# Forgetting attention: query blocks from last to first, the causal mask added by GpSimd, value products from the last keys

## The chip, the core and the metric

One Trainium2 chip, one of its cores. A core has TensorE (matrix products, into the accumulators in PSUM), VectorE, ScalarE and GpSimd for elementwise work, and SyncE, which here issues DMAs. Each runs its own instructions in the order in which they were queued; semaphores make one wait for another. The metric is device time in microseconds (us), lower is better, as the median of several runs.

## What is computed

Two layers of a hybrid decoder trunk on 528 positions: 16 learned meta tokens, then 512 real tokens; width 1024, float32. A layer norms its input, projects it once, and hands the columns to two groups of heads: 8 heads of *forgetting attention* (64 wide) and 4 heads of chunkwise retention (128 wide). Their outputs are concatenated, projected and added to the input; then comes a gated feed-forward part. The change lies in the forgetting attention:

```python
c = jnp.cumsum(logf, axis=1).transpose(0, 2, 1)      # per head, over positions
s = jnp.einsum('bhqd,bhkd->bhqk', q_blk, k_) * scale
s = s + c_q[..., :, None] - c_k[..., None, :]
s = jnp.where(k_pos[None, :] <= q_pos[:, None], s, -jnp.inf)
p = jax.nn.softmax(s, axis=-1)
out = jnp.einsum('bhqk,bhkd->bhqd', p, v_)
```

The 16 meta queries are one block, the 512 real queries four blocks of 128. In the second layer the meta queries' output is not needed, so that layer has the four real blocks alone.

## The kernel before

**Numbers in two halves.** Every float32 matrix is split into a high part (ScalarE rounds it to TensorE's fast format, line 143, or 192 for weights) and a low part (what is left, by VectorE on line 144, or by GpSimd or VectorE on line 195 for weights). A dense product is three matmuls a chunk (`dense_steps`, line 218): high times high, high times low, low times high. Weights are fetched by SyncE's queue (line 159) and converted about one job (128 output columns, eight chunks of work) before TensorE needs them.

**Order of the work.** TensorE's instructions stand in an order written out by hand: `layer` builds a plan, in which `merge` lays the steps of attention and retention between the chunks of dense products at given places, and `spread` spaces a list of steps evenly between two of them. TensorE keeps that order. For the other engines a scheduler decides the order when the program is built, by simulating it; work under `tc.high_priority()` goes first where several instructions are ready, and instructions under `pin` keep their program order. On the chip each queue is then fixed.

**Attention of a head pair `g` (two heads, `s` = 0 and 1).** There are four pairs a layer. `fox_steps` makes a list `todo` of (head, block): before the change, for each head, the meta block (-1, first layer alone), then blocks 0, 1, 2, 3. Block `b` sees 16 + 128 (b + 1) keys, so block 3 is the largest. The steps of each entry are:

- `scores(s, b)`: two matmuls a segment (line 511) put the scores into a PSUM bank from a pool of four (`psum_a`, tiles called `psa`); block 3 has two segments of 264 keys, so two banks. VectorE adds the triangular mask `msk` (0 or -1e30) onto the last 128 columns in PSUM (line 517). Then one VectorE instruction (line 518) subtracts the scores and the broadcast sums `bc` from zero, writes the result to `pr` and keeps each row's minimum; ScalarE exponentiates with that minimum and sums each row (line 531). `bc` holds a head's cumulative sums, the same row on all 128 partitions; it is fetched by a DMA (line 501) at the head's first block, into one of two buffers, from `cdr`, which the layer wrote to DRAM shortly before (line 403).
- `values()`, after the second scores: five transposes of the value tile (line 420, tile `pd`) into two banks, four in the first, and splits of them (lines 487, 488).
- `turn(s, b)`, three entries later: `b` + 1 transposes of 128 columns of the probabilities (line 420, tile `pr`) into one bank, then high and low halves into `pth` and `ptl` (lines 143, 144). The meta block turns on VectorE and ScalarE alone (lines 557 to 559). What sticks out over the 128-wide key tiles, the last 16 keys of each block, goes through a small VectorE transpose (line 535) and lines 565 to 567. `pr`, `pth` and `ptl` exist once, for both heads.
- `product(s)`: nine matmuls (line 584; one more for the meta queries, line 576) into one bank, over the key tiles j = 0 to 4, high and low halves (j = 4, the last 16 keys, is one matmul). Its result is gathered by lines 587 and 588. `product(0)` stands after all turns of head 0, just ahead of the first turn of head 1; `product(1)` ends the list.

Retention steps of one head (lines 672 to 793) run between these in three of the four pairs, and take banks from the same pool.

Of the kernel before, what the change touches and what calls it, by code (L numbers as in the profile page):

```python
# [10 lines left out]
F32 = mybir.dt.float32  # L11
# [19 lines left out]
NBLK = SEQ // 128  # L31
# [8 lines left out]
def hybrid_kernel(ctx, tc, x_t, w_in, w_fl, w_out, w_gate, w_up, w_down, vecs, b_fg, rope, decay, mask, ident, out_t):  # L40
    nc = tc.nc
# [12 lines left out]
    msk = const.tile([128, 128], F32, name="msk")  # L54
# [62 lines left out]
    def take(lst, key):  # L117
        t = lst[rot[key] % len(lst)]
        rot[key] += 1
        return t  # L120
# [150 lines left out]
    def at(tag, dt=F32R, shape=(128, T), bufs=None):  # L271
        return phase["att"].tile(list(shape), dt, name=tag, tag=tag, bufs=bufs)
# [200 lines left out]

    def fox_steps(g, st, ly, real):

        blocks = list(range(0 if real else -1, NBLK))
        todo = [(s, b) for s in range(2) for b in blocks]
        info = {}

        def values():  # L480
            st["v"] = [at(f"vv{s}", shape=(128, 5, 128)) for s in range(2)]
            for j0, n, p3 in transpose_into(st["vt"], KOFF):
                for s in range(2):
                    v = st["v"][s][:, j0:j0 + n]
                    a0, a1 = ROWS[s]
                    b0, b1 = ROWS[1 - s]
                    nc.scalar.copy(v[:, :, a0:a1], p3[:, :, a0:a1])
                    nc.vector.tensor_sub(v[:, :, b0:b1], p3[:, :, a0:a1], v[:, :, a0:a1].bitcast(F32))
            st["mt"] = at("mixt", F32)

        def span(b):
            nq = META if b < 0 else 128
            nk = META if b < 0 else META + 128 * (b + 1)
            return nq, nk, (0 if b < 0 else META + 128 * b)

        def scores(s, b):
            nq, nk, q0 = span(b)
            if b == blocks[0]:
                bc = at("bc", F32, bufs=2)
                hd = 2 * g + s  # L500
                nc.sync.dma_start(bc, ly["cdr"][hd:hd + 1, :].partition_broadcast(128))
                st["bc"] = bc
            bc = st["bc"]
            segs = FULL if nk == T else ((0, nk),)
            pt = take(pm_tiles, "pm") if b < 0 else p_tiles[0][:, PSTEP * b:PSTEP * b + nk]
            mins = []
            normalise()
            for c0, c1 in segs:
                sc = psum_a()
                for i, kk in enumerate(st["k"][s]):  # L510
                    nc.tensor.matmul(sc[0:nq, 0:c1 - c0], st["q"][s][:, q0:q0 + nq], kk[:, c0:c1],  # L511
                                     start=(i == 0), stop=(i == 1))
                nm = tmp.tile([128, 1], F32, name="nmax", tag="nmax", bufs=6)
                with tc.high_priority():
                    if c1 == nk:
                        diag = sc[0:nq, c1 - c0 - nq:c1 - c0]
                        nc.vector.tensor_add(diag, diag, msk[0:nq, 0:nq])
                    nc.vector.tensor_tensor_reduce(pt[0:nq, c0:c1], sc[0:nq, 0:c1 - c0], bc[0:nq, c0:c1],  # L518
                                                   -1.0, 3.0e38, ALU.add, ALU.min, nm[0:nq])
                mins.append(nm)  # L520
            nmax = mins[0]
            if len(mins) > 1:
                nc.vector.tensor_tensor(nmax, mins[0], mins[1], ALU.min)
            if b < 0:
                rsum = tmp.tile([META, 1], F32, name="rsum", tag="rsum", bufs=4)
            else:
                if (s, b) == (0, 0):
                    st["sums"] = tmp.tile([128, NBLK, 2], F32, name="sums", tag="sums")
                rsum = st["sums"][:, b, s:s + 1]
            pr = pt[0:nq, 0:nk]  # L530
            nc.scalar.activation(pr, pr, AF.Exp, bias=nmax[0:nq], scale=-1.0, accum_out=rsum)  # L531
            info[s, b] = pt
            if b == blocks[-1]:
                st["ends"] = at("pe", F32, (32, NBLK, 32), 2)
                nc.vector.transpose(st["ends"], ends(p_tiles[0])[96:128])
            if b < 0:
                info["open"] = (pr, rsum)
            elif (s, b) == todo[-1]:
                nc.vector.reciprocal(st["sums"], st["sums"])
                st["rows"] = tt("tq")  # L540
                nc.scalar.copy(st["rows"][:, 0:SEQ].rearrange("p (b s d) -> p b s d", b=NBLK, s=2),
                               st["sums"].unsqueeze(3).broadcast_to([128, NBLK, 2, 64]))

        def normalise():
            if "open" in info:
                pr, rs = info.pop("open")
                nc.vector.reciprocal(rs, rs)
                nc.vector.tensor_scalar_mul(pr, pr, rs)

        def turn(s, b):  # L550
            nq, nk, q0 = span(b)
            pth, ptl = t_tiles
            if (s, b) == todo[-2]:
                normalise()
            if b < 0:
                e = at("pm", F32, (128, 32))[64:96]
                nc.vector.transpose(e, info[s, b])
                nc.scalar.copy(pth[64:64 + META, 4, 0:META], e[0:META, 0:META])
                nc.vector.tensor_sub(pth[96:96 + META, 4, 0:META], e[0:META, 0:META], pth[64:64 + META, 4, 0:META].bitcast(F32))
                return  # L560
            for j0, n, p3 in transpose_into(info[s, b], [128 * j for j in range(b + 1)]):
                split(pth[:, j0:j0 + n, q0:q0 + nq], ptl[:, j0:j0 + n, q0:q0 + nq], p3[:, :, 0:nq])
            if b == blocks[-1]:
                e = st["ends"][0:META, :, 32 - META:32]
                nc.scalar.copy(corners(pth)[0:META, 1:], e)
                nc.vector.tensor_sub(corners(ptl)[0:META, 1:4], e[:, 0:3], corners(pth)[0:META, 1:4].bitcast(F32))
                nc.vector.tensor_sub(pth[32:32 + META, 4, SEQ:T], e[:, 3], pth[0:META, 4, SEQ:T].bitcast(F32))

        def product(s):
            mt, v, pt = st["mt"], st["v"][s], t_tiles  # L570
            a0, a1 = ROWS[s]
            b0, b1 = ROWS[1 - s]
            ol = tt("ol")
            if not real:
                po = psum_a()
                nc.tensor.matmul(po[:, 0:META], v[:, 4, :], pt[0][:, 4, 0:META], start=True, stop=True)
                with tc.high_priority():
                    nc.scalar.copy(ol[a0:a1, 0:META], po[b0:b1, 0:META])
                    nc.vector.tensor_add(mt[a0:a1, 0:META], po[a0:a1, 0:META], ol[a0:a1, 0:META])
            po = psum_a()  # L580
            for j in range(5):
                c0 = max(0, KOFF[j] - META)
                for i, pp in enumerate(pt if j < 4 else pt[:1]):
                    nc.tensor.matmul(po[:, c0:SEQ], v[:, j, :], pp[:, j, META + c0:T],  # L584
                                     start=(j == 0 and i == 0), stop=(j == 4))
            with tc.high_priority():
                nc.scalar.copy(ol[a0:a1, META:T], po[b0:b1, :])
                nc.vector.tensor_add(mt[a0:a1, META:T], po[a0:a1, :], ol[a0:a1, META:T])
            if s == 1:

                rb = psum_a()
                for b in range(NBLK):
                    nc.tensor.transpose(rb[:, 128 * b:128 * b + 128], st["rows"][:, 128 * b:128 * b + 128], idt)
                nc.vector.tensor_mul(mt[:, META:T], rb, mt[:, META:T])
                mh, ml = mix_tile(2 * (g % 2))
                split(sv(mh, real), sv(ml, real), sv(mt, real))
                st["mix"] = (mh, ml)

        steps = []
        n = len(todo)  # L600
        lag = 3
        for i in range(n + lag):
            if i < n:
                steps.append(lambda a=todo[i]: scores(*a))
            if i == 1:
                steps.append(values)
            if i >= lag:
                s, b = todo[i - lag]
                if s == 1 and b == blocks[0]:
                    steps.append(late(lambda: product(0)))  # L610
                steps.append(lambda a=(s, b): turn(*a))
        steps.append(lambda: product(1))
        cut = len(steps) - lag - 1
        return steps[:cut], steps[cut:]
# [810 lines left out]
```

## Time and profile before

| what | value |
|---|---|
| runs shown (median, lowest, highest) | 1272.59 us (1272.03 to 1273.82), 3 runs |
| span of the profiled execution, first to last instruction | 1270.1 us |
| median of the runs less that span | 2.5 us |
| TensorE busy | 1252.6 us (99%) |
| VectorE busy | 1003.8 us (79%) |
| ScalarE busy | 694.5 us (55%) |
| GpSimd busy | 263.3 us (21%) |
| mean granted TensorE clock | 0.996 of full speed |

The profiled execution has no time of its own beside its span; the span is compared with the median. A row of a group reads: line, engine, operation, tiles (out<-in), shape, count, busy time, mean of one in ns, idle time of the engine just ahead of it and what ended that. A row of the timeline reads: start, length, engine, line, operation, tiles, shape, count, and in brackets the idle time ahead of it. PE is TensorE's matmuls, PEld its weight loads, DVE VectorE, ACT ScalarE, POOL GpSimd, SP SyncE; SPq marks a DMA being issued. Matmuls overlap, so one may last 0.28 us while the next starts 0.12 us after it.

### The profile page before, as it was taken

What the parts mean: (1) busy time and instruction counts of PE and PEld (TensorE: products, weight loads), DVE (VectorE), ACT (ScalarE), POOL (GpSimd) and SP (SyncE); (2) the same over time, 40 slices, a digit from 0 to 9 for tenths busy, and PEclk for the clock granted to TensorE, in tenths of its full rate; (3) what the DMA queues carried; (4) which work ended last, traced back from release to release, by engine and by line L of the source; (5) the groups of instructions that cost most, each with busy time, mean ns of one, the idle gap of its engine ahead of it and who ended that gap; (6) DMA issues with size and microseconds to landing.
All of it is one profiled execution on the core that took longest, in us unless ns stands there. A gap on an engine that the chain in (4) does not pass through costs nothing.

```text
span 1270.1 us, 23589 instructions
## 1 busy us (share of the span) xinstructions
PE 1252.6 (99%) x9225; PEld 1193.1 (94%) x9225; DVE 1003.8 (79%) x1866; ACT 694.5 (55%) x1284; POOL 263.3 (21%) x524
## 2 busy tenths in 40 slices
PE   9999999999999999999999999999999999999997
PEld 8899999999999999999998989998789999999996
DVE  7877856879988888887786877568899888888867
ACT  7666556676444444444465665457764444444445
POOL 3355546420000000000025546454100000000000
PEclk9999999999999999999999999999999999999999
DMA  6322222213323232322323122221223333333321
GB/s 218 93 68 84 83 94 75 68 68 116 106 96 100 100 100 100 100 100 84 101 76 114 63 101 84 77 91 67 100 91 126 101 100 101 100 100 100 100 84 67
DMA packets 45679, 120.56 MB, mean 95 GB/s; under 512 B 5360, under 2 KB 12272, under 8 KB 45568
## 3 DMA queue, kind: packets, MB, share of 16 engines
q1 hardware_dynamic: 45136, 118.77, 28.3%
q8 instruction: 72, 1.18, 0.4%
q14 instruction: 39, 0.32, 0.1%
q10 hardware_dynamic: 432, 0.29, 0.1%
HBM read 116.91 MB, written 2.13 MB: 94 GB/s over the span
## 4 chain that ended last, share of the span: by engine, by line
PE 89%; DVE 5%; ACT 4%; DMA 1%; issue 1%; ACTq 0%; DVEq 0%; SPq 0%
PE psd L218 27%; PE psa L902 18%; PE psd L1037 14%; PE psd L902 13%; PE psa L218 5%; PE psa L1037 4%; PE psa L420 2%; PE psa L511 1%; PE psa L584 1%; PE psa L717 1%; PE psa L751 1%; DMA bc<-cdr 1%; PE psa L381 1%; ACT whi L192 1%; DVE pr L518 0%
## 5 line engine op out<-in xcount | busy, mean ns | idle before, releaser
L195 POOL TENSOR_TENSOR wlo<-raw,whi 128x128 fp32r<-128x128 f32 x504 | 259.1, 550 | 288.8 <-ACT whi L192 287.3
L218 PE MATMUL psd<-xh,whi 128*128 128x264 f32 (+1 forms) x792 | 195.6, 314 | 0.4 <-ACT whi L192 0.4
L218 PE MATMUL psd<-xl,whi 128*128 128x264 f32 (+1 forms) x792 | 186.3, 302 | 0.6 <-DVE xl L321 0.6
L218 PE MATMUL psd<-xh,wlo 128*128 128x264 f32 (+1 forms) x792 | 186.7, 303 | 0.0
L218 PEld LDWEIGHTS psd<-xh,whi 128*128 128x128 f32 x792 | 128.2, 189 | 5.2 <-ACT whi L192 0.8
L218 PEld LDWEIGHTS psd<-xh,wlo 128*128 128x128 f32 x792 | 127.0, 188 | 6.3 <-DVE wlo L195 0.6
L218 PEld LDWEIGHTS psd<-xl,whi 128*128 128x128 f32 x792 | 127.6, 189 | 5.2 <-DVE xl L321 1.2
L192 ACT CAST whi<-raw 128x512 fp32r<-128x512 f32 (+1 forms) x168 | 98.2, 613 | 45.7 <-PE psd L218 31.5
L890 ACT CAST whi<-raw 128x1024 fp32r<-128x1024 f32 (+2 forms) x62 | 54.8, 884 | 50.3 <-PE psd L902 37.0
L890 ACT CAST fwhi<-raw 128x1024 fp32r<-128x1024 f32 (+2 forms) x62 | 55.6, 897 | 47.9 <-PE psd L902 40.1
L891 DVE TENSOR_TENSOR fwlo<-raw,fwhi 128x1024 fp32r<-128x1024 f32 (+2 forms) x62 | 64.0, 1032 | 11.7 <-ACT fwhi L890 11.6
L85 POOL MEMSET kl<- 64x528 f32 x2 | 1.1, 534 | 345.5 <-PE psa L902 345.5
L891 DVE TENSOR_TENSOR wlo<-raw,whi 128x1024 fp32r<-128x1024 f32 (+2 forms) x62 | 62.9, 1014 | 12.2 <-ACT whi L890 12.1
L902 PE MATMUL psa<-th,whi 128*128 128x264 f32 (+1 forms) x232 | 65.4, 282 | 0.0
L902 PE MATMUL psa<-th,wlo 128*128 128x264 f32 (+1 forms) x232 | 65.4, 282 | 0.0
L902 PE MATMUL psa<-tl,whi 128*128 128x264 f32 (+1 forms) x232 | 65.3, 282 | 0.0
L902 PE MATMUL psa<-th,fwhi 128*128 128x264 f32 (+1 forms) x224 | 63.4, 283 | 0.0
L902 PE MATMUL psa<-tl,fwhi 128*128 128x264 f32 (+1 forms) x224 | 63.3, 283 | 0.0
L902 PE MATMUL psa<-th,fwlo 128*128 128x264 f32 (+1 forms) x224 | 63.2, 282 | 0.0
L531 ACT ACTIVATE pr<-pr,nmax 128x144 f32<-128x144 f32 (+1 forms) x64 | 36.9, 576 | 43.2 <-DVE nmax L518 31.2
L890 ACT CAST fwhi<-S 128x1024 fp32r<-128x1024 f32 x20 | 21.0, 1049 | 68.6 <-PE psa L902 66.5
L968 ACT COPY e<-psa 128x264 f32<-128x264 f32 (+1 forms) x114 | 42.9, 376 | 27.7 <-PE psa L902 23.6
(356 smaller groups left out, 4036.6 us busy)
## 6 DMA issues: line engine op xcount, KB each, us to landing
raw<-w_in SPq DMA_DIRECT2D x54, 512.0 KB, 3.5
raw<-w_gate SPq DMA_DIRECT2D x44, 512.0 KB, 4.0
fraw<-w_up SPq DMA_DIRECT2D x38, 512.0 KB, 3.4
raw<-w_down SPq DMA_DIRECT2D x64, 256.0 KB, 2.7
raw<-w_out SPq DMA_DIRECT2D x16, 512.0 KB, 3.4
raw<-w_down SPq DMA_DIRECT2D x32, 192.0 KB, 2.5
bc<-cdr SPq DMA_DIRECT2D x16, 264.0 KB, 3.4
raw<-w_up SPq DMA_DIRECT2D x6, 512.0 KB, 3.5
```

Of the source, the lines that this page charges most:

```text
L192: pin(nc.scalar.copy(hi, job["raw"][:, c0:c1]), pinned)
L195: pin(sub(lo[:, c:c + step], job["raw"][:, c0 + c:c0 + c + step], hi[:, c:c + step].bitcast(F32)), pinned)
L218: nc.tensor.matmul(ps[1][b][:, 0:c1 - c0], w[:, wk, :], x[:, c0:c1], start=(k == 0 and i == 0), stop=(k == n - 1 and i == 2))
L381: nc.tensor.matmul(ps[:, 0:c1 - c0], wf[k // HB][:, k % HB, :], st["x"][k][part][:, c0:c1], start=(i == 0), stop=(i == 2 * NK - 1))
L420: nc.tensor.transpose(ps[:, 128 * j:128 * j + 128], src[:, o:o + 128], idt)
L511: nc.tensor.matmul(sc[0:nq, 0:c1 - c0], st["q"][s][:, q0:q0 + nq], kk[:, c0:c1], start=(i == 0), stop=(i == 1))
L531: nc.scalar.activation(pr, pr, AF.Exp, bias=nmax[0:nq], scale=-1.0, accum_out=rsum)
L890: nc.scalar.copy(hi, src)
L891: nc.vector.tensor_sub(lo, src, hi.bitcast(F32))
L902: nc.tensor.matmul(bank()[:, 0:b.shape[-1]], a[:, o + k, :], b, start=(fresh and k == 0 and i == 0), stop=(k == n - 1 and i == 2), skip_gr ...
L968: nc.scalar.copy(self.t["e"][:, i], self.t["x"][:, 0:w])
L1037: nc.tensor.matmul(v[:, 0:c1 - c0], a[:, s * n + k, :], b[:, c0:c1], start=(k == 0 and i == 0), stop=(k == n - 1 and i == 2))
```

## The change

Three things. The blocks of a head go from 3 down to 0 (and to the meta block in the first layer); places that named the first, the last or a certain entry of the list are named anew. The mask is no longer added to each score tile in PSUM by VectorE: a new `mask(b)` lets GpSimd add it to the columns of `bc` that are block `b`'s own keys, at the head's start for block 3 and right after block `b`'s scores for block `b` - 1. Since later (smaller) blocks never read the columns that were masked for larger ones, one `bc` serves all blocks. And `product` runs over j = 4, 3, 2, 1, 0 where it ran 0 to 4.

```diff
-        blocks = list(range(0 if real else -1, NBLK))
+        blocks = list(range(NBLK - 1, -1 if real else -2, -1))
...
+        def mask(b):
+            nq, nk, q0 = span(b)
+            diag = st["bc"][0:nq, nk - nq:nk]
+            with tc.high_priority():
+                nc.gpsimd.tensor_add(diag, diag, msk[0:nq, 0:nq])
+
         def scores(s, b):
             nq, nk, q0 = span(b)
             if b == blocks[0]:
-                bc = at("bc", F32, bufs=2)
+                st["bc"] = at("bc", F32, bufs=2)
                 hd = 2 * g + s
-                nc.sync.dma_start(bc, ly["cdr"][hd:hd + 1, :].partition_broadcast(128))
-                st["bc"] = bc
+                nc.sync.dma_start(st["bc"], ly["cdr"][hd:hd + 1, :].partition_broadcast(128))
+                mask(b)
             bc = st["bc"]
...
                 with tc.high_priority():
-                    if c1 == nk:
-                        diag = sc[0:nq, c1 - c0 - nq:c1 - c0]
-                        nc.vector.tensor_add(diag, diag, msk[0:nq, 0:nq])
                     nc.vector.tensor_tensor_reduce(pt[0:nq, c0:c1], sc[0:nq, 0:c1 - c0], bc[0:nq, c0:c1],
                                                    -1.0, 3.0e38, ALU.add, ALU.min, nm[0:nq])
                 mins.append(nm)
+            if b > blocks[-1]:
+                mask(b - 1)
...
-                if (s, b) == (0, 0):
+                if (s, b) == todo[0]:
                     st["sums"] = tmp.tile([128, NBLK, 2], F32, name="sums", tag="sums")
...
-            if b == blocks[-1]:
+            if b == 0:
                 st["ends"] = at("pe", F32, (32, NBLK, 32), 2)
...
-            elif (s, b) == todo[-1]:
+            elif (s, b) == (1, 0):
                 nc.vector.reciprocal(st["sums"], st["sums"])
...
-            if b == blocks[-1]:
+            if b == 1:
                 e = st["ends"][0:META, :, 32 - META:32]
...
-            for j in range(5):
+            for j in range(4, -1, -1):
                 c0 = max(0, KOFF[j] - META)
                 for i, pp in enumerate(pt if j < 4 else pt[:1]):
                     nc.tensor.matmul(po[:, c0:SEQ], v[:, j, :], pp[:, j, META + c0:T],
-                                     start=(j == 0 and i == 0), stop=(j == 4))
+                                     start=(j == 4), stop=(j == 0 and i == 1), skip_group_check=True)
```

## The prediction

> **What bounds the kernel now.** I read the page's busy line, then the same shares in the stretches that hold attention (20 to 330 us in layer 0, 640 to 960 us in layer 1), then who made TensorE wait there.
>
> ```profile
> span 1270.1 us, 23589 instructions
> PE 1252.6 (99%) x9225; PEld 1193.1 (94%) x9225; DVE 1003.8 (79%) x1866; ACT 694.5 (55%) x1284; POOL 263.3 (21%) x524
> ...
> 20.00:330.00 310.00, 305.60 (x2466) 301.88 (x2465) 244.75 (x572) 196.63 (x433) 128.84 (x248) 0.99 0.26 85
> 640.00:960.00 320.00, 317.48 (x1980) 283.43 (x1979) 245.34 (x516) 197.65 (x405) 130.27 (x256) 1.00 0.26 86
> ```
> ```profile
> PE psa L584 <- DVE ptl L144: 1.7, 1, 1.7
> PE psa L511 <- DVE mixt L588: 0.7, 1, 0.7
> PE psa L511 <- DVE kl L454: 0.6, 1, 0.6
> PE psa L511 <- DVE nmax L518: 0.6, 1, 0.6
> ...
> PE psa L420 <- DVE vv L488: 1.6, 1, 1.6
> ```
>
> The columns of the two stretches are length, then busy time of PE, PEld, DVE, ACT, POOL, then granted clock. TensorE works 305.6 of 310 us and 317.5 of 320 us, and the change takes no matmul from it and adds none. So it can win only TensorE's waits, and the second fence holds nearly all of those in the attention part (the last row is layer 1, the others layer 0). VectorE has 65 and 75 us to spare in these stretches, GpSimd 181 and 190 us: work that leaves the one for the other is worth nothing by itself.
>
> The longest wait is the first product with values, 1.69 us, and TensorE's clock shows more:
>
> ```profile
> 55.50 0.59 ACT L143 CAST pth<-psa 128x512 fp32r<-128x512 f32 x1
> 56.63 0.48 PE L584 MATMUL psa<-pth,vv 128*128 128x512 f32 x1
> 58.06 0.68 DVE L144 TENSOR_TENSOR ptl<-psa,pth 128x512 fp32r<-128x512 f32 x1
> 58.79 0.51 PE L584 MATMUL psa<-ptl,vv 128*128 128x512 f32 x1 [1.69 <-DVE ptl L144]
> ...
> 75.17 0.48 PE L584 MATMUL psa<-pth,vv 128*128 128x512 f32 x1
> 75.48 0.39 PE L584 MATMUL psa<-ptl,vv 128*128 128x512 f32 x1
> ...
> 59.20:60.60 1.40, 1.40 (x8) 0.54 0.40 79
> 60.60:62.70 2.10, 2.10 (x11) 0.50 0.49 197
> ```
>
> The low half of the last block's transposed probabilities (512 columns) came at 58.74, with TensorE already there. The same pair of matmuls starts 2.16 us apart here and 0.31 us apart without a wait, so the wait is worth 1.85 us. Then the granted clock was 0.54 and 0.50 for 3.5 us: 1.40 x 0.46 + 2.10 x 0.50 = 1.69 us. Together 3.54 us, the largest thing that this change can reach.
>
> **The change, part by part.**
>
> *Order of blocks and of the product's keys.* Today the block before the product is the heaviest: four transposes (52.90 us below) and a 512-column split. Reversed, the last turned blocks are block 0 (one transpose, one 128-column split) and, in layer 0, the meta block (no TensorE work). Block 0's turn moves to where block 2's stands (50.13).
>
> ```profile
> 45.80 0.27 PE L420 MATMUL psa<-idt,pr 128*128 128x128 f32 x1
> 49.52 0.28 DVE L144 TENSOR_TENSOR ptl<-psa,pth 128x128 fp32r<-128x128 f32 x1
> 50.13 0.49 PE L420 MATMUL psa<-idt,pr 128*128 128x128 f32 x3
> 52.90 0.60 PE L420 MATMUL psa<-idt,pr 128*128 128x128 f32 x4
> ```
>
> With block 0's own lag, 45.80 to 49.80 = 4.0 us, its low half would be there at 54.1, 2.5 us before the product (56.63); the product also reads key block 0 last, some 0.8 us later still (1648 columns stand ahead of it, and layer 0's mean is 305.6 us / 2466 = 0.124 us for about 264). So this wait goes, and the half clock behind it: -3.54 us. Next in line there is the meta block's chain (normalise, transpose, split), which needs no TensorE and has about four steps, at 1.4 us each by the two turns above (50.13, 52.90: two steps); I cost it at nothing, and at 1 us if VectorE's backlog of some 4 us covers it too. The nine matmuls of a product are the same nine in another order: nothing.
>
> *Waits for a PSUM bank.*
>
> ```profile
> 240.87 0.39 PE L511 MATMUL psa<-kh,qs 128*128 128x264 f32 x1 [0.69 <-DVE mixt L588]
> ...
> 104.06 0.41 PE L218 MATMUL psd<-xh,wlo 128*128 128x264 f32 x2
> 104.62 0.41 PE L420 MATMUL psa<-idt,pr 128*128 128x128 f32 x2
> ...
> 104.39 0.16 DVE L517 TENSOR_TENSOR psa<-psa,msk 16x16 f32<-16x16 f32 x1
> ```
>
> After a product, scores waited 0.69 us for its bank. Scores of two banks follow the product today, and are replaced by a turn of one bank and a one-bank score. I take the 0.69 us as gone; bounds 0 and 0.69.
>
> *The mask leaves VectorE for GpSimd.*
>
> ```profile
> L517 DVE TENSOR_TENSOR psa<-psa,msk x72: 160/290/300, 36.7 to 863.4; 128x128 f32<-128x128 f32 x64, 16x16 f32<-16x16 f32 x8
> ...
> 20.00:330.00 310.00, 10.59 (x40) 0.99 0.26 85
> 640.00:960.00 320.00, 9.36 (x32) 1.00 0.26 86
> ...
> L195 POOL TENSOR_TENSOR wlo<-raw,whi x504: 446/463/2074, 21.6 to 897.8; 128x128 fp32r<-128x128 f32 x168
> L518 DVE CUSTOM_DVE_ANT_0 pr<-psa,bc x80: 289/432/575, 39.6 to 864.6; 128x264 f32<-128x264 f32 x32, 128x144 f32<-128x144 f32 x16, 128x272 f32<-128x272 f32 x16, 128x400 f32<-128x400 f32 x16
> ```
>
> VectorE loses 72 instructions, 10.59 + 9.36 = 19.95 us, all under TensorE's work: 0, except the start at 104.62 us above, right behind a mask's end (104.55) and 0.44 us after the matmul before it (104.18) where 0.124 is usual: -0.3. GpSimd gains 64 sums of 128x128, nearest row L195: 64 x 0.46 to 0.55 (the median and the page's mean) = 30 to 35 us, in idle time. But each sum is now a hand-over: the reduction L518 of block b must have read the columns before GpSimd masks them for b-1, and L518 of b-1 waits for that. With two hand-overs of 0.05 us (58.74 to 58.79 above) that is 0.65 us at most, and scores of one head are two steps, some 2.8 us, apart except at its start. So it hides, as long as GpSimd comes to it within about 2 us. Behind the mask on GpSimd stand the low halves of the weights (L195), converted about a job ahead, some 5 us; behind L518 on VectorE stands everything.
>
> *The start of a pair's attention.* Block 3 comes first and takes two of four banks at once, block 2 a third, the values' transposes a fourth and then a fifth. The hard places are the two layer starts, where the broadcast sums have just been fetched:
>
> ```profile
> 37.05 3.38 POOL L195 TENSOR_TENSOR wlo<-raw,whi 128x128 fp32r<-128x128 f32 x8 [5.66 <-ACT whi L192]
> 37.60 0.71 PE L420 MATMUL psa<-idt,pd 128*128 128x128 f32 x5
> 39.44 0.16 DVE L518 CUSTOM_DVE_ANT_0 pm<-psa,bc 16x16 f32<-16x16 f32 x1 [1.72 <-DMA bc<-cdr]
> 39.67 0.40 PE L511 MATMUL psa<-kh,qs 128*128 128x272 f32 x1 [0.62 <-DVE nmax L518]
> ...
> 675.95 0.31 DVE L518 CUSTOM_DVE_ANT_0 pr<-psa,bc 128x144 f32<-128x144 f32 x1 [2.95 <-DMA bc<-cdr]
> 680.09 0.30 PE L420 MATMUL psa<-idt,pd 128*128 128x128 f32 x1 [1.57 <-DVE vv L488]
> ```
>
> Layer 0: TensorE reaches the fifth transpose at 37.60 + 0.7 (1536 more columns of scores, at 0.124 us per 264) + 0.5 (four transposes of 0.12) = 38.8, and its bank is free only after block 3's first reduction, 39.44 + 0.43 + 0.1 = 40.0: a wait of 1.2 us where 0.62 stands. If the mask gets behind the eight L195 (to 40.43), the second reduction ends at 41.5 and costs 0.4 more. I take +0.8 (bounds +0.2, +2.5, the latter with a half clock again). Layer 1: by the same count the fifth transpose meets a free bank at 676.5, and the later waits for the retention's values stay; 0 (bounds -1.6, +1.5). The six other starts, where the sums are there long before: +0.8 for all, about 0.13 each (0 to 0.55, one L195, each). SyncE: the fetch of the sums still waits for a head's last reduction, now of a small block; I take 0.
>
> Sum: -3.54 - 0.69 - 0.3 + 0.8 + 0 + 0.8 = -2.9 us on the span, 1270.1 to 1267.2. The median of the runs shown, 1272.59, lies 2.5 us above the span; I carry that over: **1269.6 us**.
>
> [...]
>
> **Rivals.**
>
> *Slower: GpSimd's queue holds VectorE up.* GpSimd runs in order and waited long for ScalarE:
>
> ```profile
> POOL wlo L195 <- ACT whi L192: 287.3, 74, 32.3
> ...
> 45.81 2.07 POOL L195 TENSOR_TENSOR wlo<-raw,whi 128x128 fp32r<-128x128 f32 x4 [5.38 <-ACT whi L192]
> 47.49 0.95 DVE L627 TENSOR_TENSOR xsw<-xsw,sr 128x528 f32<-128x528 f32 x1 [0.34 <-ACT xsw L626]
> ...
> 55.51 0.71 DVE L627 TENSOR_TENSOR xsw<-xsw,sr 128x528 f32<-128x528 f32 x1 [1.29 <-ACT xsw L626]
> ```
>
> A mask placed behind a low half whose high half is late keeps L518, and VectorE behind it, waiting. If that costs TensorE one L195 (0.55 us) a head, 16 heads make 8.8 us: 1278.4. It decides from (2.9 + 2.5) / 16 = 0.34 us a head. For it: 74 waits of L195 for ScalarE. Against: VectorE's 140 us of slack, and the steps' spacing. A second brake of the same kind: L627, with two SBUF inputs, took 0.71 us alone and 0.95 beside L195, so a mask can add some 0.24 us to such an instruction; at 64 masks that is 15 us of VectorE at most, less than the 20 it loses. [...]
>
> *Same: the wait moves.* The half clock comes back at layer 0's start, where I expect 1.2 us of waiting: +1.69 us and a little more waiting give 1271.5 to 1273.5, middle 1272.6. That the reversal does nothing, since the meta block's chain is late in the old wait's place, ends there too.
>
> *Better:* all bank waits of the fence go, 1.57 and 0.62 included, and the starts cost nothing: -3.54 - 0.69 - 0.3 - 2.2 = -6.7, 1265.9.
>
> **How the numbers follow.** 0.2% is 2.5 us, about what a measurement of this kernel tells from no change: faster is under 1270.05. Likeliest case 0.42 (own range 1267.5 to 1271.5, three quarters of it faster), better 0.11, the wait moves 0.18, the clock's loss not coming back 0.03, slower 0.26. Faster 0.43, same 0.31, slower 0.26. The range 1265 to 1279 leaves out the far ends of better and of slower.
>
> **What would show it.** Right: no L584 waiting on L144 near 58 us, clock 1.00 from 55 to 66 us; no adds on VectorE at the mask's line, 72 on GpSimd near 0.46 to 0.55 us; a TensorE wait of over 1 us near 39 us. Wrong: rows of L518 waiting for GpSimd that sum to many us, TensorE waiting at scores or turns in most heads, or a slice of low clock at a layer's start.

## The result and the profile after

The changed kernel takes 1288.81 us (median, 1288.22 to 1290.69) against 1272.31 us (1271.31 to 1273.82) for the kernel before, measured beside it: a ratio of 1.0131, 95% interval 1.0117 to 1.0144. It is 16.5 us slower. Forecast was 1269.6 us, and the range ended at 1279.

The first two lines of the page after, span and busy time of each engine:

```profile
span 1288.9 us, 23656 instructions
...
PE 1259.9 (98%) x9225; PEld 1196.4 (93%) x9225; DVE 992.0 (77%) x1794; ACT 695.7 (54%) x1284; POOL 294.9 (23%) x596
```

TensorE does the same 9225 matmuls, and is busy 7.3 us longer for them (1252.6 before). Some 5 us of that are a lower clock: it is granted at 0.50 for four stretches of 3.41 us where it was one, and 3 x 3.41 x 0.5 = 5.1 us. Where the other 2 us of busy time come from isn't shown. The remaining 11.5 us of the longer span (1288.9 against 1270.1) are TensorE's waits. VectorE has 72 instructions less and GpSimd 72 more, as the diff says. The waits of VectorE and GpSimd, then those of TensorE (what waited, for what: us in total, times, longest):

```profile
POOL bc L500 <- DVE nmax L521: 25.1, 23, 4.4
...
DVE pr L521 <- POOL bc L500: 20.2, 16, 2.6
...
POOL bc L500 <- DMA bc<-cdr: 14.6, 5, 4.6
...
PE psa L420 <- DVE mixt L584: 4.1, 2, 3.0
...
PE psa L517 <- DVE ptl L144: 2.6, 3, 1.8
...
PE psa L420 <- DVE nmax L521: 2.1, 2, 1.3
...
PE psa L420 <- DVE vv L488: 1.9, 1, 1.9
...
PE psa L517 <- DVE nmax L521: 1.3, 2, 1.0
```

The 1.69 us wait of the first product is gone, as forecast. In its place stand turns that wait for a bank behind a product's meta queries (4.1 us; line 584 is the old 576's result), and scores and turns that wait for splits and reductions. Behind these stands VectorE, which waits 16 times, 20.2 us together, in the reduction (line 521, the old 518) for a mask by GpSimd (line 500). One such place, in the timeline of the changed kernel (start, length, engine, line; in brackets the idle time ahead):

```profile
746.03 2.98 POOL L195 TENSOR_TENSOR wlo<-raw,whi 128x128 fp32r<-128x128 f32 x7 [2.05 <-ACT whi L192]
...
746.44 0.43 DVE L521 CUSTOM_DVE_ANT_0 pr<-psa,bc 128x272 f32<-128x272 f32 x1
...
748.98 0.45 POOL L500 TENSOR_TENSOR bc<-bc,msk 128x128 f32<-128x128 f32 x1
...
749.46 0.31 DVE L521 CUSTOM_DVE_ANT_0 pr<-psa,bc 128x144 f32<-128x144 f32 x1 [2.58 <-POOL bc L500]
...
749.83 0.39 PE L517 MATMUL psa<-kh,qs 128*128 128x264 f32 x1 [0.96 <-DVE nmax L521]
...
752.19 0.39 PE L517 MATMUL psa<-kh,qs 128*128 128x264 f32 x1 [1.84 <-DVE ptl L144]
...
752.60:756.10 3.50, 3.50 (x13) 2.81 (x13) 2.98 (x11) 1.75 (x5) 1.80 (x4) 0.51 0.27 101
```

At 746.03 GpSimd starts seven low halves of weights (line 195), which had waited 2.05 us for ScalarE. At 746.88 VectorE has finished the larger block's reduction (746.44 and its minimum, 0.08 us, behind it), so from then on the next mask could run. It stands behind the low halves in GpSimd's queue and starts at 748.98, when the last of them is done, without a gap. VectorE stands still for 2.58 us. TensorE then waits 0.96 us at the next scores, and 1.84 us more for a split that VectorE does late. The last row is the stretch behind (length, then busy time of PE, PEld, DVE, ACT, POOL, then the granted clock): the clock is 0.51 for 3.5 us, some 1.7 us more. Twelve of the other fifteen waits of that row look the same: GpSimd comes to the mask straight from a run of low halves. The other three, 1.4 us together, are at the two layer starts, with no low half just ahead of the mask.

The second new kind of wait, from the same view:

```profile
244.63 0.16 DVE L584 TENSOR_TENSOR mixt<-psa,ol 64x16 f32<-64x16 f32 x1
...
244.94 1.08 PE L420 MATMUL psa<-idt,pr 128*128 128x128 f32 x4 [3.02 <-DVE mixt L584]
```

and two stretches behind it, in the same columns:

```profile
245.00:248.60 3.60, 3.60 (x17) 3.60 (x18) 2.90 (x6) 0.59 (x1) 0.00 (x0) 0.50 0.45 150
248.60:252.00 3.40, 3.40 (x22) 3.32 (x21) 1.15 (x4) 0.41 (x2) 0.00 (x0) 0.66 0.00 0
```

In layer 0's last pair the first head's product is followed by block 3's turn, whose four transposes need a bank. The banks are taken until VectorE has gathered the product's meta columns at 244.63, so TensorE waits 3.02 us, and its clock is 0.50 and 0.66 for 7 us: 3.6 x 0.50 + 3.4 x 0.34 = 3.0 us more. Before, this place cost 0.69 us.

The time between fixed points of TensorE's list shows where all of it went. A pair ends, in this table, with the first of the four transposes by which its row sums are turned for the scaling (tiles `psa<-idt,tq`); starts are read from each trace and subtracted. Differences to the kernel before in us, one profiled execution each (the one of the changed kernel is the slowest of its four runs, so its sum is 18.8):

| stretch | changed | mask back | order alone | meta first | first pair only |
|---|---|---|---|---|---|
| to the first scores | -0.2 | +0.1 | -0.3 | -0.1 | +0.1 |
| layer 0, pair 1 | -0.5 | -2.9 | -3.1 | -1.9 | -3.0 |
| pair 2 | +2.7 | +1.4 | +1.4 | -0.1 | -0.1 |
| pair 3 | +1.7 | -0.2 | -0.2 | +0.1 | +0.1 |
| pair 4 | +5.0 | +5.5 | +3.6 | +0.4 | 0.0 |
| to layer 1's scores | +0.5 | +0.4 | +0.6 | +1.0 | 0.0 |
| layer 1, pair 1 | +3.8 | +2.3 | +2.0 | +2.3 | 0.0 |
| pair 2 | +4.9 | 0.0 | 0.0 | 0.0 | 0.0 |
| pair 3 | +1.4 | 0.0 | 0.0 | 0.0 | 0.0 |
| pair 4 and the rest | -0.4 | +0.3 | +0.3 | +0.4 | +0.1 |

The last four columns are kernels of the experiments below.

### The profile page after: what moved, and what is told of

It reads as the page before. It is cut to its first block, busy times and chain, and to the rows that moved or that the text cites. A ratio compares the mean times of both kernels' runs of the same rounds, so it can differ in the third digit from the quotient of the medians.

```text
span 1288.9 us, 23656 instructions
## 1 busy us (share of the span) xinstructions
PE 1259.9 (98%) x9225; PEld 1196.4 (93%) x9225; DVE 992.0 (77%) x1794; ACT 695.7 (54%) x1284; POOL 294.9 (23%) x596
## 4 chain that ended last, share of the span: by engine, by line
PE 81%; DVE 7%; ACT 6%; POOL 2%; issue 2%; DMA 1%; ACTq 0%; DVEq 0%; SPq 0%; POOLq 0%
PE psd L218 23%; PE psa L907 18%; PE psd L1042 14%; PE psd L907 13%; PE psa L1042 4%; PE psa L218 4%; POOL wlo L195 2%; PE psa L420 1%; ACT whi L192 1%; PE psa L517 1%; PE psa L589 1%; PE psa L722 1%; PE psa L756 1%; PE psa L381 1%; DVE kl L454 1%
## 5 line engine op out<-in xcount | busy, mean ns | idle before, releaser
L536 ACT ACTIVATE pr<-pr,nmax 128x272 f32<-128x272 f32 (+2 forms) x64 | 36.9, 576 | 52.2 <-DVE nmax L521 34.1
L521 DVE CUSTOM_DVE_ANT_0 pr<-psa,bc 128x264 f32<-128x264 f32 (+3 forms) x80 | 33.6, 433 | 38.0 <-POOL bc L500 20.2
```

## The experiments

**Which part costs.** Three kernels undo one part each, or keep one alone; a fourth keeps the product's order alone. The masks back on VectorE:

```diff
-        def mask(b): ...                 (and its two calls)
+                    if c1 == nk:
+                        diag = sc[0:nq, c1 - c0 - nq:c1 - c0]
+                        nc.vector.tensor_add(diag, diag, msk[0:nq, 0:nq])
```

> The changed kernel with one part undone: the mask is again added to the scores in PSUM by VectorE; blocks still go from last to first, products still begin at the last keys. Theory A (the slowdown is the hand-over between VectorE and GpSimd: VectorE waited 20 us for masks): all of the 16.5 us goes, 1269 to 1274 us. Theory B (the slowdown is the order of the blocks, which asks for more PSUM banks at a pair's start and right after the product): 1283 to 1289 us. Half and half would be about 1280 us.

The product back to j = 0 to 4, masks and order as changed:

```diff
-            for j in range(4, -1, -1):
+            for j in range(5):
```

> The changed kernel with the product's key order undone (0 to 4 again); GpSimd masks and reversed blocks stay. Theories A and B: 1288 us within 2, the same nine matmuls wait for the same tiles. Theory C (the product's order costs): 1285 us or less.

The reversed blocks alone, in the kernel before:

```diff
-        blocks = list(range(0 if real else -1, NBLK))
+        blocks = list(range(NBLK - 1, -1 if real else -2, -1))
```

> The reversed order of blocks alone: VectorE masks the scores in PSUM, products go from the first keys. Theory A: 1269 to 1274 us. Theory B: 1283 to 1289 us. If the product's order matters for the reversed blocks, this differs from the kernel with both by over 1 us.

The reversed product alone, in the kernel before:

```diff
-            for j in range(5):
+            for j in range(4, -1, -1):
```

> The kernel before with the product's key order reversed alone. Theories A and B: 1272 us within 1; the long wait at the first product stays, since the first keys' low half of block 3 is late for each key tile alike. Theory C: slower than 1274 us.

Measured beside 1271.5 us of the kernel before: masks back 1276.44 us (1.0041, 1.0027 to 1.0055), product back 1288.4 us (1.0134, 1.0119 to 1.015), order alone 1276.28 us (1.0035, 1.002 to 1.0049), product alone 1271.84 us (1.0002, 0.9992 to 1.0011). "Mask back" and "order alone" fall between the ranges of theories A and B: both the masks and the order cost. The product's order does nothing, the blocks' order loses 4.8 us (1276.28 - 1271.5), and the masks the rest: "product back" differs from "order alone" by the masks only, 1288.4 - 1276.3 = 12.1 us. The table says where: the order gains 3.1 us in layer 0's first pair and loses 7 in three other places; the masks add their 12 us in six of the eight pairs.

**Is it GpSimd's work, or the wait for it?** A kernel with the masks on VectorE, as in "mask back", in which GpSimd still does the 72 additions, one a block and of the same inputs, into a tile that nobody reads:

```diff
-                nc.gpsimd.tensor_add(diag, diag, msk[0:nq, 0:nq])
+                nc.gpsimd.tensor_add(idle[0:nq, 0:nq], diag, msk[0:nq, 0:nq])
+                    (and VectorE's addition to the scores, as before)
```

> Reversed order, the mask added to the scores by VectorE, and GpSimd does the same 72 sums besides, into a tile that nobody reads. Theory A1: nobody waits for them, 1275 to 1279 us. [...]

It took 1278.12 us (1.0052, 1.0039 to 1.0066). The two pages' lines of busy time, of "mask back" and of this one:

```profile
PE 1256.3 (98%) x9225; PEld 1195.7 (94%) x9225; DVE 1004.0 (79%) x1866; ACT 695.6 (54%) x1284; POOL 262.3 (21%) x524
```
```profile
PE 1256.1 (98%) x9225; PEld 1195.4 (94%) x9225; DVE 1005.7 (79%) x1866; ACT 695.7 (54%) x1284; POOL 295.5 (23%) x596
```

GpSimd works 33.2 us more (295.5 against 262.3), VectorE 1.7 us more, and the ratios' intervals overlap. So the 72 additions on GpSimd, while nobody waits for them, do not make the 12 us: had they done so, this kernel would stand near 1288.5 us (1276.44 + 12.1). Of the up to 15 us that the prediction allowed for VectorE instructions slowed beside a mask, 1.7 us show here.

**Does it have to be GpSimd's queue?** Two kernels move the wait. In the first, VectorE itself adds the masks to the sums:

```diff
-                nc.gpsimd.tensor_add(diag, diag, msk[0:nq, 0:nq])
+                nc.vector.tensor_add(diag, diag, msk[0:nq, 0:nq])
```

> The changed kernel with one engine exchanged: the mask is added to the broadcast sums as in the change, block by block after the block before, but by VectorE. Theory A1 (the cost of the mask is that VectorE waits while GpSimd has it in its queue): near the kernel with the mask on the scores, 1275 to 1279 us. Theory A2 (the cost is the chain itself: a mask can only follow the reduction of the block before, whatever the engine): 1284 to 1289 us.

In the second, each block has its own copy of the sums, fetched and masked at the head's start, so no mask waits for a reduction:

```diff
-                st["bc"] = at("bc", F32, bufs=2)
-                nc.sync.dma_start(st["bc"], ...)
-                mask(b)
+                for a in range(NBLK - 1, -1, -1):
+                    n = span(a)[1]
+                    st["bc"][a] = at(f"bc{a}", F32, (128, n), 1)
+                    nc.sync.dma_start(st["bc"][a], ly["cdr"][hd:hd + 1, 0:n].partition_broadcast(128))
+                    mask(a)
```

> The changed kernel with the chain taken away: the sums are fetched once for each of the four blocks, and GpSimd masks each copy as soon as it has landed, a head ahead (only the meta block's mask still follows block 0). The order and the engine stay. Theory A1 and A2: VectorE's 20 us of waiting for masks fall under 6, and the time to 1274 to 1280 us. [...] If the three further fetches a head hold up SyncE's queue, VectorE waits for the fetches instead, over 1282 us.

Both stayed where the changed kernel is: 1288.2 us (1.0133, 1.0119 to 1.0147), the range of theory A2, and 1290.33 us (1.0146, 1.0128 to 1.0164), where A1 and A2 had 1274 to 1280. Their waits, first of the kernel with VectorE's masks, then of the one with a copy for each block:

```profile
DVE bc L500 <- DMA bc<-cdr: 27.4, 11, 7.9
...
PE psa L420 <- DVE nmax L521: 5.3, 3, 2.0
```
```profile
POOL bc L500 <- DMA bc<-cdr: 78.8, 31, 4.8
...
PE psd L218 <- POOL wlo L195: 4.7, 4, 2.1
...
DVE pm L524 <- POOL bc L500: 7.6, 4, 5.1
...
DVE pr L524 <- POOL bc L500: 3.0, 4, 1.2
```

In the first, GpSimd is out of it, but a head's first mask stands in VectorE's queue at the place that the scheduler gave it and waits there for the sums' fetch: 11 times, 27.4 us. In the second, VectorE's waits for masks fall only to 10.6 us, not under the 6 expected: 3.0 us at the four blocks, and 7.6 us at the meta block (tile `pm`), whose mask still follows block 0. GpSimd waits 78.8 us for the fetches (each copy's single buffer is free only after the head before); the low halves behind it come late, and TensorE waits 4.7 us for them where it waited for none. In all three forms an instruction whose input isn't there holds up what stands behind it in its queue: in the changed kernel low halves that wait for ScalarE (2.05 us at 746.03) hold up the mask, here VectorE's masks wait 27.4 us and GpSimd's 78.8 us for the fetches. But since the first landed in A2's range, these two could not tell whether the form itself (masks on the sums) is dear, so a third was made: the kernel with VectorE's masks, but a head's first block masked in the scores, so that nothing waits for the fetch ahead of its reader.

```diff
-                mask(b)                  (at a head's first block)
+                    if c1 == nk and b == blocks[0]:
+                        diag = sc[0:nq, c1 - c0 - nq:c1 - c0]
+                        nc.vector.tensor_add(diag, diag, msk[0:nq, 0:nq])
```

> The changed kernel, but VectorE itself adds the masks to the sums of every block but a head's first, and the first block's mask is added to the scores, as in the kernel before. No mask stands in GpSimd's queue and none waits for the sums' fetch. If the 12 us of the mask part belong to masks that wait in somebody's queue (for a row of low halves on GpSimd in the changed kernel, for the fetch on VectorE in the vector-masks-sums kernel), this one stands where the mask-back kernel stands: 1275 to 1279 us. If they belong to the form itself (a mask on the sums orders each head's blocks one behind the other), it stays with the changed kernel: 1284 us or more. In between: both have a share.

1278.03 us (1.0055, 1.004 to 1.007); the interval overlaps that of "mask back" (1.0041, 1.0027 to 1.0055). So A2 fails: the form costs nothing that these runs tell apart. The 10 us between 1288.2 and 1278.0 go with the first mask of each head, the one that waited for the fetch in VectorE's queue.

**The queue made short.** The low halves cut to 8 of 128 columns, in the changed kernel, in "mask back" and in the kernel before. TensorE's third product takes the high half in place of the low one, so it does as many matmuls; the output lacks the low halves' part.

```diff
-                pin(sub(lo[:, c:c + step], raw[:, ...], hi[:, c:c + step]), pinned)
+                m = 8 if job["pool"] else 128
+                pin(sub(lo[:, c:c + step, 0:m], raw[:, ..., 0:m], hi[:, c:c + step, 0:m]), pinned)
...
-                for i, (w, x) in enumerate(((hi, xh), (hi, xl), (lo, xh))):
+                for i, (w, x) in enumerate(((hi, xh), (hi, xl), (hi if pool else lo, xh))):
```

> The changed kernel, with GpSimd's row of low halves (L195) cut to 8 of 128 columns each, so that the queue ahead of its masks is nearly empty; the third product of those weights takes the high half in place of the low one, so its output lacks the low halves' part, and TensorE does as many products as before. To be read against the next kernel, which is the mask-back kernel with the same cut. If the masks' price is the wait behind the low halves, the two differ by 0 to 3 us; if it is the hand-over to GpSimd, or GpSimd's slowness as such, by about 12 us as the uncut pair does (1288.8 against 1276.4 us).

> The mask-back kernel (reversed blocks, reversed product, masks added to the scores by VectorE) with GpSimd's low halves cut to 8 of 128 columns and the high half in the third product of those weights, so its output lacks the low halves' part. Without a mask on GpSimd the low halves are early anyway, so 1274 to 1278 us is expected, by either theory; it is the base for the kernel before this one.

> The kernel before with GpSimd's low halves cut to 8 of 128 columns and the high half in the third product of those weights, so its output lacks the low halves' part. The light mask-back kernel took 1269.0 us, which was 7.4 us below the uncut one; this one tells how much of that was GpSimd's low halves for any kernel. If the cut is worth the same to the kernel before, it takes 1264 us, and the order still costs 5 us; if the order's loss itself needs the low halves, it takes 1269 to 1271 us.

Measured: changed and cut 1268.83 us (0.9981, 0.9972 to 0.9991), mask back and cut 1268.99 us (0.9984, 0.9975 to 0.9993), before and cut 1264.97 us (0.9948, 0.9931 to 0.9964). "Mask back and cut" was expected at 1274 to 1278 us, so that expectation was wrong: the cut takes some 7 us off that kernel too. Of the first, the group of low halves and the waits for masks:

```profile
L196 POOL TENSOR_TENSOR wlo<-raw,whi 128x8 fp32r<-128x8 f32 x504 | 104.2, 241 | 318.5 <-ACT whi L192 309.7 <-issue 8.7
```
```profile
POOL bc L501 <- DVE nmax L522: 53.1, 38, 4.5
...
DVE pr L522 <- POOL bc L501: 6.7, 10, 1.5
```

One low half takes 241 ns where it took 545, and a run of them is short. The masks are handed over as before, 72 times; they now wait mostly for VectorE (53.1 us), and VectorE for them 6.7 us, with no wait over 1.5. And the 12.1 us are gone: 1268.83 against 1268.99. So the hand-over as such costs nothing here; the masks' price needs the low halves around them in GpSimd's queue. The cut also shortens VectorE's own work, by 17 us (986.7 against 1004.0 us busy in the two "mask back" kernels), which eases all waits for VectorE; that the queue is how the price comes about is read from the rows of 746 to 752 us, not from the cut alone. Nor does it separate a mask that waits behind low halves from low halves that wait behind a mask; for the first speaks that TensorE's list of waits in the changed kernel has no row for GpSimd's low halves. The cut is worth 5.7 us to the kernel before as well, so the order's loss, 4.8 us uncut, is 4.0 us here (1268.99 - 1264.97): the order doesn't need the low halves for it.

**What the order loses.** The reversed blocks put block 3's turn right behind the first head's product. The kernel with the order alone has, in layer 0's last pair:

```profile
238.80 0.16 DVE L578 TENSOR_TENSOR mixt<-psa,ol 64x16 f32<-64x16 f32 x1
238.88 0.67 DVE L587 TENSOR_TENSOR mixt<-psa,ol 64x512 f32<-64x512 f32 x1
...
239.01 0.66 PE L420 MATMUL psa<-idt,pr 128*128 128x128 f32 x4 [2.41 <-DVE mixt L578]
```

a wait of 2.41 us. If that is the loss, leaving the meta rows first (meta, 3, 2, 1, 0) takes it away, since the turn behind the product is then the meta block's, without a bank:

```diff
-        blocks = list(range(NBLK - 1, -1 if real else -2, -1))
+        blocks = ([] if real else [-1]) + list(range(NBLK - 1, -1, -1))
```

> The kernel before with the blocks of a head reversed, as in the order-alone kernel (1276.3 us), except that the 16 meta rows of layer 0 stay first: meta, 3, 2, 1, 0. The first turn behind the first head's product is then the meta block's, which takes no PSUM bank. If the loss of 3.6 us in layer 0's last pair is the turn of block 3 that waits for the bank of the meta product, it goes: 1272 to 1274 us, with about +2 us left at the start of layer 1, which is not touched. If the loss comes from the reversed blocks elsewhere, it stays at 1276. If the gain of 3 us in the first pair came from the meta rows' new place, that goes too and the time is 1275 to 1279.

1273.75 us (1.0017, 1.0008 to 1.0027), within the first theory's 1272 to 1274. The same place, in this kernel's timeline:

```profile
236.22 0.16 DVE L578 TENSOR_TENSOR mixt<-psa,ol 64x16 f32<-64x16 f32 x1
...
241.46 0.60 PE L420 MATMUL psa<-idt,pr 128*128 128x128 f32 x4
```

The transposes wait for nothing, and the stretch costs 0.4 us where it cost 3.6; pair 2 has lost its 1.4 us too. What stays is the start of layer 1, +2.3 us. There the fifth transpose of the retention's values waits for a bank that still holds the attention's transposed values, until ScalarE and VectorE have split those (lines 487 and 488). First rows of this kernel, then its clock in the stretch behind, then that of the kernel before:

```profile
678.17 0.63 ACT L530 ACTIVATE pr<-pr,nmax 128x400 f32<-128x400 f32 x1
...
678.91 0.49 ACT L487 CAST vv<-psa 128x256 fp32r<-128x256 f32 x2
...
679.32 0.56 DVE L488 TENSOR_TENSOR vv<-psa,vv 128x256 fp32r<-128x256 f32 x2 [1.19 <-ACT vv L487]
...
680.75 0.30 PE L420 MATMUL psa<-idt,pd 128*128 128x128 f32 x1 [1.90 <-DVE vv L488]
```
```profile
681.70:685.10 3.40, 3.40 (x13) 2.71 (x12) 3.02 (x10) 2.33 (x8) 0.00 (x0) 0.50 0.13 41
```
```profile
681.70:685.10 3.40, 3.40 (x26) 3.14 (x25) 2.87 (x10) 2.18 (x5) 1.52 (x3) 1.00 0.22 59
```

Before, that wait was 1.57 us and no clock was lost. VectorE isn't what is late: it stands still for 1.19 us until ScalarE starts the split at 678.91. ScalarE does the exponentials of blocks 3 and 2 just ahead of it (0.73 and 0.63 us), where before it was block 1's alone (0.52 us). The wait is 1.90 us, and the clock falls to 0.50 for 3.4 us: 1.7 us, most of the 2.3.

**The gain alone.** The order gains in one pair and loses in others, so a last kernel reverses the blocks in layer 0's first pair and leaves all else as before:

```diff
+        if g == 0 and not real:
+            blocks.reverse()
```

> The kernel before with the blocks reversed in one pair alone, the first of layer 0, masks and product as before. In the run with the order alone that pair was 3.05 us shorter and the others longer or alike. If pairs are independent: 3 us off the span, 1268 to 1269.5 us against 1271.5 us. Rival: what the order saves there comes back in the pairs behind it, 1271 us or more.

1268.96 us beside 1270.51 us of the kernel before, ratio 0.998, interval 0.9971 to 0.9988: 0.2% faster, and within the expected 1268 to 1269.5. Its first product, and its clock behind it:

```profile
57.51 0.48 PE L586 MATMUL psa<-pth,vv 128*128 128x512 f32 x1
...
57.83 0.39 PE L586 MATMUL psa<-ptl,vv 128*128 128x512 f32 x1
```
```profile
59.00:66.00 7.00, 7.00 (x61) 6.86 (x60) 6.16 (x19) 5.65 (x14) 4.95 (x10) 1.00 0.35 113
```

The high and the low half's matmuls start 0.32 us apart, the clock stays 1.00, and the pair is 3.0 us shorter.

## Why the prediction was wrong, step by step

- *Order, first product, -3.54 us:* right in mechanism and nearly in size. The wait and the half clock go, and the first pair alone gains 3.0 us of its table row. In the changed kernel the masks take 2.4 us of it back in the same pair (-0.5, against -2.9 in "mask back"); a turn there waits 1.04 us for the meta product's bank.
- *Bank behind a product, -0.69 us:* this step failed. "Scores of two banks follow the product today, and are replaced by a turn of one bank and a one-bank score" overlooked that the turn which stood there, the meta block's, takes no bank at all. In its place came waits of 4.1 us, the longest (3.02) with 3.0 us of clock behind it. With the order alone it is one wait of 2.41 us, and "meta first" takes it away.
- *The mask, -0.3 us, and its hand-over hidden:* the step that failed most. "So it hides, as long as GpSimd comes to it within about 2 us" was a condition, and the sum went on as if it held. It counted the low halves that stand behind a mask in GpSimd's queue, not those ahead of it. GpSimd came up to 2.6 us late, TensorE ran out of work meanwhile (0.96 and 1.84 us at the place shown), and the masks cost 12.1 us where the sum had -0.3. The slack of VectorE, 140 us in sum, was no argument, since the wait falls where TensorE's next step hangs on VectorE.
- *Layer 0's start, +0.8 us (wait of 1.2 us where 0.62 stood):* right within 0.2 us. The changed kernel waits 1.29 and 0.35 us there, 1.0 us more than before.
- *Layer 1's start, 0 (-1.6 to +1.5):* too low. The order alone costs 2.0 us, the changed kernel 3.8. The prediction had the retention's values wait as before; they wait 0.33 us longer in "meta first" (1.90 against 1.57), behind ScalarE's larger exponentials, and behind that the clock was 0.50 for 3.4 us; the bound had no half clock in it, though the argument for layer 0 did.
- *The six other starts, +0.8 us for all:* not told apart from the bank waits by any run; with the order alone four of the six show nothing, and with "meta first" none loses over 0.4 us.
- *The product's order, 0:* right (1.0002).
- *The rival "GpSimd's queue holds VectorE up":* this is what happened, at a chance of 0.26. It put one low half, 0.55 us, on a head; VectorE's waits were 20.2 / 16 = 1.3 us a head, since a mask stands behind a run of low halves (seven at 746.03) rather than one, and TensorE lost 12.1 / 16 = 0.76. The masks alone leave the range (1269.6 + 12.1 = 1281.7); the order's 4.8 us, which no rival had, come on top.
- *The clock:* the prediction counted 1.69 us of half clock behind a wait of 1.69 us, and gave 0.03 to "the clock's loss not coming back", a loss that stays when the wait goes. It went with the wait: in "first pair only" the clock is 1.00 from 59 to 66 us, where the kernel before has a mean of 0.76, and the pair is 3.0 us shorter, more than the 1.85 us that the wait alone was worth. At layer 1's start in "meta first" a wait of 1.90 us had 0.50 for 3.4 us behind it.

## What to carry to other kernels

An instruction given to an idle engine is not free when another engine's next instruction waits for it (12.1 us here, for 72 additions of 0.46 us in the median): count what can stand ahead of it in that engine's queue (here a run of four to eight low halves, about 2 to 4 us), not the engine's busy share, and ask what the waiting engine holds up in turn. When steps are reordered, write down for each what it takes from a shared pool at its new place; a step that took nothing and made room for a late one is easily lost. And where a reordering gains in one known place, change that place alone.

## What was not expected of the hardware

Two waits at one place differ little, and the clock behind them much: behind 1.57 us of waiting (the kernel before, layer 1) it stayed 1.00, and behind 1.90 us at the same place ("meta first") it was 0.50 for 3.4 us. A third of a microsecond more of waiting thus came with about 2 us of loss. A wait of 1.04 us in the changed kernel's first pair showed no loss (timeline, then the stretch around it with the clock in the third place from the end):

```profile
62.63 0.55 PE L420 MATMUL psa<-idt,pr 128*128 128x128 f32 x3 [1.04 <-DVE mixt L584]
```
```profile
59.00:66.00 7.00, 5.96 (x49) 5.59 (x48) 5.72 (x18) 4.59 (x13) 2.26 (x6) 1.00 0.29 91
```

and one of 3.02 us lost 3.0 us over 7 us. In the changed kernel the clock of 0.50 stands in four stretches of 3.41 us, from 244.07, 247.48, 691.22 and 752.66 us. Three stretches of that length at a clock of 1.00 (start and end, length, TensorE's busy time): the one ahead of the low clock in the kernel before, the one ahead of it in "meta first", and one in the kernel before that holds the wait of 1.57 us:

```profile
55.89:59.30 3.41, 1.72 (x12) 1.35 (x11) 3.19 (x9) 2.34 (x7) 2.19 (x4) 1.00 0.00 0
...
678.26:681.67 3.41, 1.51 (x10) 1.18 (x10) 2.02 (x8) 1.81 (x7) 0.00 (x0) 1.00 0.39 141
...
677.12:680.53 3.41, 1.84 (x12) 1.45 (x11) 1.98 (x8) 1.91 (x8) 1.70 (x4) 1.00 0.30 94
```

TensorE is idle 1.69, 1.90 and 1.57 us in them (3.41 less the busy time). The clock of the 3.4 us behind is 0.50, 0.50 and 1.00. What sets it is not shown by these rows.

With GpSimd's low halves cut, the kernel before has VectorE busy 984.4 us where it was 1003.8, with as many instructions (1866), while GpSimd works 159.3 us less (263.3 - 104.0). The first line of busy time of the cut kernel:

```profile
PE 1250.0 (99%) x9225; PEld 1192.7 (94%) x9225; DVE 984.4 (78%) x1866; ACT 695.5 (55%) x1284; POOL 104.0 (8%) x524
```

By that rate, 19.4 / 159.3, the 33.2 us of idle additions should have cost VectorE 4.0 us; they cost 1.7.
